# Putting off the gate-and-conv work of the last two up groups, and splitting and fetching the down product's operands in other slots

## The chip, the cores and the metric

The kernel runs on one core of a Trainium2 chip. The metric is the device time of one execution in microseconds (us), from its first to its last instruction and what lies around them; several executions are timed and their median is given. Engines: PE (TensorE, matrix products), DVE (VectorE), ACT (ScalarE), POOL (GpSimd), and SP (SyncE), whose instruction stream issues nearly all transfers (DMAs).

## The reference

One decoder layer on a sequence of 512 positions and width 2048, all in float32:

```python
h = rms_norm(x, norm1_w)
proj = h @ w_in                       # attention heads and an SSM scan follow
x = x + concat([attn, ssm]) @ w_out
h = rms_norm(x, norm2_w)
u = causal_dwconv(h @ w_up, ffn_conv_w, ffn_conv_b)     # 2048 -> 2 * 5632, conv over 3 positions
u_gate, u_val = split(u, 2, axis=-1)
return x + (silu(u_gate) * u_val) @ w_down              # 5632 -> 2048
```

The case is about the last two products, `h @ w_up` (the up product) and `... @ w_down` (the down product), and about the places where one gives way to the next.

## The kernel before

**Precision.** A float32 operand `a` is split into `hi`, a copy in a shorter format that PE takes at full rate (made by ACT), and `lo = a - hi` (made by DVE). A product is then three matmuls: hi·hi, hi·lo, lo·hi.

**Seven products for eight.** Both products are cut in 2 x 2 blocks and done by a scheme with seven products of sums of blocks, named `P1` to `P7`, instead of eight. For each it needs a combination of weight blocks (the left side, one of the tiles `rawa`, `rawb`, or a sum `s` of several, made by DVE and held in PSUM; one sum, in SBUF, `s3`, is made by POOL on line 1027) and a combination of the activations (the right side). The right sides are fixed for many groups; the kernel calls them "kinds" (`KT1, K11, KT2, K21, KT3, K22, KT4`) and holds each as one tile `cmb0` to `cmb6` with hi and lo, with one buffer each.

**Groups and slots.** The up product has 44 groups (`NF = 44`), each a group of output columns with n = 8 blocks of depth. The down product has three passes over the depth (`PASSES`: 7, 8 and 7 pairs of blocks, so n = 7, 8, 7), each with 8 groups. One product of one group is a slot, of 3n matmuls of 128 x 256. `put` (lines 1007 to 1009) interleaves neighbours: seven slots in the order `P5(g), P3(g-1), P1(g), P4(g-1), P6(g), P2(g), P7(g)`. At the first group of a pass the kinds have to be new ones, so each kind's tile is written anew between its last use by the old groups and its first use by the new ones.

**The order of the work.** The slots are issued in order (lines 1284 to 1306), and the order on the other engines is written out by hand: after a slot's matmuls come the reading of its result (`up_after` or `down_after`), and then `step_slot(slot)`: the list `events` of this slot (weight loads, the sums `s2`, `s4`, fetches), `split_lo(slot + 2)` on DVE, the list `after` of this slot (sum `s1`, kind splits, side work), and `split(slot + 3)` on ACT. Each engine works through its own instructions in the order in which they were issued. `base` is the slot of `P5` of the last group before a pass; below, r is a slot's number counted from `base`. There are three such places: from up to pass 0 (base 299), from pass 0 to pass 1 (355), from pass 1 to pass 2 (411).

**The kinds of a pass.** The up product's results, gated and summed into the kinds, lie in DRAM (`gd`). Each kind of a pass is fetched in two halves, so there are 14 halves per pass, numbered q = 0 to 13 in the order of the kinds above: `b_load` (line 1095, on SP) fetches a half into a buffer `ld` (the first two of the first pass into buffers `acc_s`), `b_split` splits it into the kind's tile (ACT line 1106, DVE line 1107). `slots` gives the slots of the splits from `base` on; fetches of the first `early` halves are issued ahead of `base`, the others one slot after the split that frees their buffer.

**Side work.** After `P4` of an up group, `up_side` issues on DVE and ACT what the layer does with the result: scale by the norm (line 1220, 1221), the conv (1198 on ACT, 1199 on DVE), SiLU (1204), gate times value (1210), and for each odd group the sums of a pair (`t_sums`: 888 to 891) and its store to `gd` (line 1067, on SP). It is spread over the seven slots after `P4`, the pair's sums over slots 7 to 10 after it, and 11 (for the last pair 8 and 9) for sums and store.

**Down results.** `down_after` adds a group's seven results up in a buffer (`acc_s` of two, or `acc` of four), and POOL issues a transfer that accumulates it onto `x2d` in DRAM (line 1170). The up product's small tiles lie in a pool `up`, which `down_pool` closes for the pool `down`.

Of the kernel before, what the change touches and what calls it, by code (L numbers as in the profile page):

```python
# [33 lines left out]
NF = FF // 128  # L34
# [17 lines left out]
PASSES = [(0, 7), (7, 8), (15, 7)]  # L52
# [137 lines left out]
def body(ctx, tc, xT, wi, wz, wo, wu, wd0, wd1, wd2, pp, pf, outT, dbg={}):  # L190
# [93 lines left out]
    def pc(name, i=0, n=1):  # L284
        o = _PC[name] + i
        return (p2["par"] if name[0] == "f" else par)[:, o:o + n]
# [513 lines left out]
    for half in range(2):  # L800
        box = {}
# [83 lines left out]
    def sums(E, g, part=None):  # L885

        if part != 1:
            E.tensor_tensor(g[:, 4:6, :], g[:, 1:4:2, :], g[:, 0:2, :], op=OP.subtract)
        if part != 0:
            E.tensor_tensor(g[:, 6, :], g[:, 3, :], g[:, 4, :], op=OP.subtract)  # L890
            E.tensor_tensor(g[:, 7, :], g[:, 2, :], g[:, 6, :], op=OP.subtract)
# [45 lines left out]
    for i in range(4, NK):  # L937
        box = {}
# [41 lines left out]
    ve, se, pe, po, sy = nc.vector, nc.scalar, nc.tensor, nc.gpsimd, nc.sync  # L980
# [3 lines left out]
    def side_tile(pool, shape, name, bufs=1):  # L984
        return pool.tile([128] + shape, F32, name=name, bufs=bufs)
# [13 lines left out]
    items, pos = [], {}  # L999
# [64 lines left out]
    events, after = {}, {}  # L1064

    def at(slot, fn, *args, where=events):
        where.setdefault(slot, []).append(lambda: fn(*args))

    for gi in range(len(groups)):
        p5, p1 = pos[gi, "P5"], pos[gi, "P1"]  # L1070
# [11 lines left out]
    gd = [dram.tile([128, n, 8, 256], F32, name="gd%d" % p) for p, (f, n) in enumerate(PASSES)]  # L1082
# [26 lines left out]
    def down_pool():  # L1109
        up_stack.close()  # L1110
        box["pool"] = ctx.enter_context(tc.tile_pool(name="down", bufs=1, side="right", reuse_waits="tile"))
        box["depth"] = 5

    for p in range(len(PASSES)):
        g0 = NF + 8 * p
        base = pos[g0 - 1, "P5"]
        slots = [2, 4, 5, 7, 8, 9, 9, 10, 11, 11, 12, 13, 14, 15]
        k0 = len(b_list)
        b_list += [(p, t, h) for t in (KT1, K11, KT2, K21, KT3, K22, KT4) for h in range(2)]
        early = 5  # L1120
        for q in range(14):
            at(base + slots[q], b_split, k0 + q, where=after)
        for q in range(14):
            at(base - 6 + q // 2 if q < early else base + slots[q - (5 if p else 3)] + 1, b_load, k0 + q)
        if p == 0:
            at(base + 19, down_pool, where=after)


    x_ld = []

    def x_load(n):
        if n < 4:
            x_ld.append(side_tile(box["pool"], [4, 256], "ld", 3))
            sy.dma_start(x_ld[n], xd[:, 4 * (n % 2):4 * (n % 2) + 4, n // 2, :])

    def x_split(n):
        t, h = (K22, KT4)[n // 2], n % 2
        if h == 0:
            up_kinds[t] = cmb_tile(t)
        o = up_kinds[t][:, :, 4 * h:4 * h + 4, :]  # L1140
        se.activation(o[:, 0], x_ld[n], AF.Copy)
        ve.tensor_tensor(o[:, 1], x_ld[n], o[:, 0].bitcast(F32), op=OP.subtract)
        x_load(n + 3)
# [5 lines left out]
    box = {}  # L1149
# [25 lines left out]
    def up_after(g, x):  # L1175
        X, i = g["X"], g["i"]
        ug, uv = box["ug%d" % (i % 2)], box["uv%d" % (i % 2)]
        if x in ("P1", "P6", "P5"):
            g[x] = side_tile(box["pool"], [256], "c" + x, 2 if x == "P5" else 1)
            se.activation(g[x], X[:, 256:] if x == "P5" else X[:, :256], AF.Copy)  # L1180
        elif x == "P2":
            ve.tensor_tensor(ug[:, 2:258], g["Y"][:, :256], g["P1"], op=OP.add)
        elif x == "P7":
            ve.tensor_tensor(uv[:, 258:514], X[:, :256], g["P5"], op=OP.add)
        elif x == "P3":
            ve.tensor_tensor(ug[:, 258:514], X[:, 256:], g["P6"], op=OP.add)
        else:
            ve.tensor_tensor(uv[:, 2:258], X[:, :256], rbc[:, :256], op=OP.mult)
            up_side(i, ug, uv)

    def up_side(i, ug, uv):
        pool = box["pool"]
        tt = {}

        def conv(u, ci, name, n):
            if n == 0:
                tt[name] = side_tile(pool, [S], name)
                se.activation(tt[name], u[:, 2:514], AF.Identity, bias=pc("fcb", ci), scale=pc("fcw", ci * 3 + 2))
            ve.scalar_tensor_tensor(tt[name], u[:, n:n + S], pc("fcw", ci * 3 + n), tt[name],
                                    op0=OP.mult, op1=OP.add)  # L1200

        def val0():
            conv(uv, NF + i, "tv", 0)
            se.activation(tt["tg"], tt["tg"], AF.Silu)

        def last():
            if i % 2 == 0:
                box["gt"] = side_tile(pool, [8, 256], "gt")
            o = 2 * (i % 2)
            ve.tensor_tensor(box["gt"][:, o:o + 2, :].rearrange("p a b -> p (a b)"), tt["tg"], tt["tv"], op=OP.mult)  # L1210

        def t_sums(n):
            sums(ve, box["gt"], n)
            if n:
                pr = i // 2
                p = max(q for q in range(3) if PASSES[q][0] <= pr)
                at(t0 + (11 if i < NF - 1 else 9), sy.dma_start, gd[p][:, pr - PASSES[p][0]], box["gt"])

        t0 = pos[i, "P4"]
        for d, fn in ((0, lambda: ve.tensor_tensor(ug[:, 2:514], ug[:, 2:514], rbc, op=OP.mult)),  # L1220
                      (1, lambda: ve.tensor_tensor(uv[:, 258:514], uv[:, 258:514], rbc[:, 256:], op=OP.mult)),
                      (3, lambda: conv(ug, i, "tg", 0)), (4, lambda: conv(ug, i, "tg", 1)), (5, val0),
                      (6, lambda: conv(uv, NF + i, "tv", 1)), (6, last)):
            at(t0 + d, fn, where=after)
        if i % 2:
            at(t0 + 7, t_sums, 0, where=after), at(t0 + (10 if i < NF - 1 else 8), t_sums, 1, where=after)

    def down_acc(gi):
        g = groups[gi]
        m, p = g["m"], g["p"]  # L1230
        if gi < NF + 2:
            a = g["acc"] = side_tile(lp, [2, S], "acc_s", 2)
        else:
            a = g["acc"] = side_tile(box["pool"], [2, S], "acc", 4)
        if p == 2:
            sy.dma_start(a, x2d[m])

    for gi, g in enumerate(groups):
        if g["ph"] == "down":
            p5 = pos[gi, "P5"]  # L1240
            at(p5 - 2 if gi == NF else p5 - 5 if gi == NF + 1 else p5 - 2 if gi == NF + 2 else p5 - 6, down_acc, gi,
               where=after)


    up_stack = ExitStack()
# [1 line left out]
    def start_up():  # L1247

        work.close()
        p2["cmb2"] = ctx.enter_context(tc.tile_pool(name="cmb2", bufs=1, side="right", reuse_waits="tile"))  # L1250
        box["pool"] = up_stack.enter_context(tc.tile_pool(name="up", bufs=1, side="right", reuse_waits="tile"))
        box["depth"] = 3
        for n in ("ug0", "uv0", "ug1", "uv1"):
            box[n] = box["pool"].tile([128, 516], F32, name=n)
            ve.memset(box[n][:, 0:2], 0.0)
        x_load(0), x_load(1), x_load(2)
# [27 lines left out]
    for k, (gi, x) in enumerate(items):  # L1284
        g = groups[gi]
        if x == "P5":
            g["X"] = box["ps"].tile([128, 512], F32, name="x")
        if x == "P2":
            g["Y"] = box["ps"].tile([128, 512], F32, name="y")
        out = g["Y"][:, :256] if x == "P2" else g["X"][:, 256:] if x in ("P5", "P3") else g["X"][:, :256]  # L1290
        h, l = parts.pop(k)
        bk = g["kinds"][KIND[x]]
        n = g["n"]
        fresh = x in ("P5", "P2")
        for part in ((range(n - 1), range(n - 1, n)) if k < 2 else (range(n),)):
            for q in part:
                w = h[:, q * 128:(q + 1) * 128]
                pe.matmul(out, w, bk[:, 0, q, :], start=fresh and q == 0, stop=False, skip_group_check=True)  # L1298
                pe.matmul(out, w, bk[:, 1, q, :], start=False, stop=False, skip_group_check=True)  # L1299
            for q in part:  # L1300
                pe.matmul(out, l[:, q * 128:(q + 1) * 128], bk[:, 0, q, :], start=False, stop=q == n - 1,  # L1301
                          skip_group_check=True)
        if k == 0:
            start_up()
        (up_after if g["ph"] == "up" else down_after)(g, x)
        step_slot(k)
# [23 lines left out]
```

## Time and profile before

| | |
|---|---|
| median of 3 runs | 2070.68 us (2070.02 to 2075.01) |
| profiled execution | 2073.51 us, its span 2071.8 us |
| granted PE clock over the span | 0.997 of full speed |
| PE busy | 2037.1 us (98%) |
| DVE busy | 1555.5 us (75%) |
| ACT busy | 1004.8 us (48%) |
| POOL busy | 223.3 us (11%) |
| DMA | 319.79 MB, mean 154 GB/s |

A row of a timeline gives the start, the duration, the engine, the line, and what is written from what; a bracket tells how long the engine stood idle before it, and for whom. On DVE the end of one instruction overlaps the start of the next by about 0.1 us, so the price of an instruction in a busy stretch is the distance from its start to the next one's. A row of a window table gives busy time and count of each engine, the granted PE clock, the share of the DMA engines that was busy, and GB/s. A row of the waits gives total, times and the longest.

### The profile page before, as it was taken

The numbers are of one execution on the slowest core, as the hardware profiler recorded it, in microseconds if no ns is written. First come the engines' busy times: TensorE is split into PE (matmuls) and PEld (weight loads), VectorE is DVE, ScalarE is ACT, GpSimd is POOL, SyncE is SP. The second block draws the span as 40 slices with busy tenths as digits, with TensorE's granted clock in tenths as the row PEclk, the third lists the DMA queues.
The fourth block names the chain that finished last, engine by engine and source line by source line (L and its number), as shares of the span: only waits on it lengthen the run. The fifth ranks groups of instructions, "written<-read, shape, count | busy, mean of one in ns | idle before, by whom it ended". The sixth has DMA issues, their size and how long they took to land.

```text
span 2071.8 us, 37628 instructions
## 1 busy us (share of the span) xinstructions
PE 2037.1 (98%) x15350; PEld 1925.7 (93%) x15350; DVE 1555.5 (75%) x2194; ACT 1004.8 (48%) x1499; POOL 223.3 (11%) x123
## 2 busy tenths in 40 slices
PE   9999999999999998999999999999999899999999
PEld 8889888888888878999999999999999899999999
DVE  6535555345555558999999999999999977967976
ACT  6433435244444435555555555555555644644533
POOL 0020000000000001101110111111011111211210
PEclk9999999999999999999999999999999999999999
DMA  5233222332225545445444444444455667856863
GB/s 196 77 108 94 80 72 82 93 111 83 82 72 168 168 136 193 161 145 194 154 157 180 166 162 162 173 174 163 154 187 203 201 189 213 263 153 215 267 204 122
DMA packets 110940, 319.79 MB, mean 154 GB/s; under 512 B 10352, under 2 KB 34736, under 8 KB 107952
## 3 DMA queue, kind: packets, MB, share of 16 engines
q1 hardware_dynamic: 108464, 309.00, 44.2%
q0 software_dynamic: 2304, 8.39, 2.5%
q8 instruction: 120, 1.97, 0.4%
q14 instruction: 52, 0.43, 0.1%
HBM read 275.38 MB, written 41.98 MB: 153 GB/s over the span
## 4 chain that ended last, share of the span: by engine, by line
PE 92%; DVE 5%; issue 1%; ACT 1%; DMA 1%; SPq 0%; POOL 0%; DVEq 0%; ACTq 0%; POOLq 0%
PE acc L185 31%; PE x L1299 16%; PE x L1298 16%; PE x L1301 16%; PE sm L185 4%; PE y L1298 3%; PE y L1299 3%; PE y L1301 3%; DVE cmb L1107 1%; DVE lo L1060 1%; DMA ld<-gd 0%; DVE lo L185 0%; DMA raw<-wi 0%; ACT hi L1051 0%; DVE t L185 0%
## 5 line engine op out<-in xcount | busy, mean ns | idle before, releaser
L1299 PE MATMUL x<-cmb,hi 128*128 128x256 f32 x3168 | 741.9, 276 | 11.7 <-DVE cmb L1107 10.2
L1298 PE MATMUL x<-cmb,hi 128*128 128x256 f32 x3168 | 741.6, 276 | 10.3 <-ACT cP L1180 5.4
L1299 PEld LDWEIGHTS x<-cmb,hi 128*128 128x128 f32 x3168 | 595.9, 188 | 14.5 <-DVE cmb L1107 12.5
L1298 PEld LDWEIGHTS x<-cmb,hi 128*128 128x128 f32 x3168 | 595.7, 188 | 12.2 <-issue 6.2
L1301 PE MATMUL x<-cmb,lo 128*128 128x256 f32 x3168 | 426.5, 275 | 1.5 <-DVE lo L1060 1.4
L1301 PEld LDWEIGHTS x<-cmb,lo 128*128 128x128 f32 x3168 | 390.5, 188 | 1.9 <-DVE lo L1060 1.9
L185 DVE TENSOR_TENSOR lo<-raw,hi 128x512 fp32r<-128x512 f32 (+1 forms) x240 | 164.4, 691 | 238.0 <-ACT hi L185 228.4
L1051 ACT ACTIVATE hi<-s 128x1024 fp32r<-128x1024 f32 (+1 forms) x201 | 201.1, 1001 | 224.4 <-DVE s L1034 151.7
L1027 POOL TENSOR_TENSOR rawb<-rawa,rawb 128x1024 f32<-128x1024 f32 (+1 forms) x68 | 170.9, 2513 | 1077.0 <-DVE s L1034 894.0
L185 PE MATMUL acc<-A,hi 128*128 128x512 f32 x704 | 278.3, 395 | 0.6 <-ACT hi L185 0.6
L185 PE MATMUL acc<-A,lo 128*128 128x512 f32 x704 | 274.2, 390 | 0.0
L185 PE MATMUL acc<-B,hi 128*128 128x512 f32 x704 | 274.2, 390 | 0.0
L185 ACT ACTIVATE hi<-raw 128x512 fp32r<-128x512 f32 (+1 forms) x240 | 149.2, 629 | 247.3 <-PE acc L185 211.6
L1060 DVE TENSOR_TENSOR lo<-s,hi 128x1024 fp32r<-128x1024 f32 (+1 forms) x201 | 238.7, 1187 | 28.7 <-issue 25.8
L1060 DVE TENSOR_TENSOR lo<-rawa,hi 128x1024 fp32r<-128x1024 f32 (+1 forms) x204 | 242.1, 1187 | 20.3 <-PE x L1301 18.7
L1051 ACT ACTIVATE hi<-rawa 128x1024 fp32r<-128x1024 f32 (+1 forms) x204 | 210.1, 1030 | 12.8 <-PE x L1299 12.7
L185 PEld LDWEIGHTS acc<-A,lo 128*128 128x128 f32 x704 | 132.6, 188 | 28.6 <-DVE lo L185 0.6
L185 PEld LDWEIGHTS acc<-A,hi 128*128 128x128 f32 x704 | 132.9, 189 | 26.3 <-ACT hi L185 0.9
L185 PEld LDWEIGHTS acc<-B,hi 128*128 128x128 f32 x704 | 132.8, 189 | 25.6
L1180 ACT ACTIVATE cP<-x 128x256 f32<-128x256 f32 x132 | 50.8, 385 | 205.1 <-PE x L1301 205.1
L185 PE MATMUL acc<-hi,A 128*128 128x256 f32 (+2 forms) x448 | 134.4, 300 | 0.8 <-DVE u L185 0.8
L185 PE MATMUL acc<-lo,A 128*128 128x256 f32 (+2 forms) x448 | 132.7, 296 | 0.0
(209 smaller groups left out, 2773.6 us busy)
## 6 DMA issues: line engine op xcount, KB each, us to landing
rawa<-wu SPq DMA_DIRECT2D x176, 512.0 KB, 3.7
raw<-wi SPq DMA_DIRECT2D x79, 512.0 KB, 3.6
rawa<-wd SPq DMA_DIRECT2D x64, 448.0 KB, 4.1
rawb<-wu SPq DMA_DIRECT2D x44, 512.0 KB, 4.5
gd<-gt SPq DMA_DIRECT2D x22, 1024.0 KB, 4.4
raw<-wo SPq DMA_DIRECT2D x32, 512.0 KB, 3.7
rawa<-wd SPq DMA_DIRECT2D x32, 512.0 KB, 4.2
ld<-gd SPq DMA_DIRECT2D x27, 512.0 KB, 7.0
```

The costliest lines, as they stand in the source:

```text
L185: return fn(out, *args, **kw)
L1027: po.tensor_tensor(r, raw[gi, "11"][:, :n], r, op=OP.subtract)
L1051: se.activation(h[:, :n], src[:, :n], AF.Copy)
L1060: ve.tensor_tensor(l[:, :n], src[:, :n], h[:, :n].bitcast(F32), op=OP.subtract)
L1107: ve.tensor_tensor(lo, ld[:, :m, :], hi.bitcast(F32), op=OP.subtract)
L1180: se.activation(g[x], X[:, 256:] if x == "P5" else X[:, :256], AF.Copy)
L1298: pe.matmul(out, w, bk[:, 0, q, :], start=fresh and q == 0, stop=False, skip_group_check=True)
L1299: pe.matmul(out, w, bk[:, 1, q, :], start=False, stop=False, skip_group_check=True)
L1301: pe.matmul(out, l[:, q * 128:(q + 1) * 128], bk[:, 0, q, :], start=False, stop=q == n - 1, skip_group_check=True)
```

## The change

Four things are edited.

1. The side work of groups 42 and 43 starts at r = 15 and r = 22 instead of at the `P4` of its group (r = 3 and r = 10). The pair sums of groups 40 and 41 go to r = 13 and 14 (before 3 and 6), their store to r = 15 (before 7); the sums of groups 42 and 43 to r = 29 and 30 (before 17 and 18), the store to r = 31 (before 19).
2. In all three passes the 14 halves are split in the slots 1, 2, 3, 4, 5, 6, 7, 8, 9, 10, 10, 11, 12, 13 instead of 2, 4, 5, 7, 8, 9, 9, 10, 11, 11, 12, 13, 14, 15.
3. Seven halves instead of five are fetched ahead, one for each slot from r = -9 to -3 (before two each in -6 and -5, one in -4). The ring of `ld` has 5 buffers in the pool `up` (before 3) and 7 in the pool `down` (before 5).
4. `down_pool` moves from r = 19 to r = 33. Groups 46 and 47 therefore take the two `acc_s` buffers in turn with groups 44 and 45 (before, they took `acc` buffers); the buffer of a down group is named two slots before its `P5`, in pass 2 six.

```diff
-        box["depth"] = 5
+        box["depth"] = 7
...
-        slots = [2, 4, 5, 7, 8, 9, 9, 10, 11, 11, 12, 13, 14, 15]
+        slots = [1, 2, 3, 4, 5, 6, 7, 8, 9, 10, 10, 11, 12, 13]
...
-        early = 5
+        early = 7
         for q in range(14):
             at(base + slots[q], b_split, k0 + q, where=after)
         for q in range(14):
-            at(base - 6 + q // 2 if q < early else base + slots[q - (5 if p else 3)] + 1, b_load, k0 + q)
+            at(base - 9 + q if q < early else base + slots[q - (7 if p else 5)] + 1, b_load, k0 + q)
         if p == 0:
-            at(base + 19, down_pool, where=after)
+            at(base + 33, down_pool, where=after)
...
-            x_ld.append(side_tile(box["pool"], [4, 256], "ld", 3))
+            x_ld.append(side_tile(box["pool"], [4, 256], "ld", 5))
...
-                at(t0 + (11 if i < NF - 1 else 9), sy.dma_start, gd[p][:, pr - PASSES[p][0]], box["gt"])
-
-        t0 = pos[i, "P4"]
+                at(t2 + (4 if i < NF - 3 else 2), sy.dma_start, gd[p][:, pr - PASSES[p][0]], box["gt"])
+
+        t1 = pos[i, "P4"]
+        if i >= NF - 2:
+            t1 = pos[NF - 1, "P5"] + (15 if i == NF - 2 else 22)
...
-            at(t0 + d, fn, where=after)
+            at(t1 + d, fn, where=after)
         if i % 2:
-            at(t0 + 7, t_sums, 0, where=after), at(t0 + (10 if i < NF - 1 else 8), t_sums, 1, where=after)
+            t2 = t1 + 7 if i != NF - 3 else pos[NF - 1, "P5"] + 13
+            at(t2, t_sums, 0, where=after), at(t2 + (3 if i < NF - 3 else 1), t_sums, 1, where=after)
...
-        if gi < NF + 2:
+        if gi < NF + 4:
             a = g["acc"] = side_tile(lp, [2, S], "acc_s", 2)
...
-            p5 = pos[gi, "P5"]
-            at(p5 - 2 if gi == NF else p5 - 5 if gi == NF + 1 else p5 - 2 if gi == NF + 2 else p5 - 6, down_acc, gi,
-               where=after)
+            at(pos[gi, "P5"] - (6 if g["p"] == 2 else 2), down_acc, gi, where=after)
...
-        box["depth"] = 3
+        box["depth"] = 5
```

## The prediction

> **What bounds the kernel now.** I read the page's busy times first, then who PE waited for, then window by window where it stood still.
>
> ```profile
> PE 2037.1 (98%) x15350; PEld 1925.7 (93%) x15350; DVE 1555.5 (75%) x2194; ACT 1004.8 (48%) x1499; POOL 223.3 (11%) x123
> ...
> PE x L1298 <- ACT cP L1180: 5.4, 2, 5.0
> ...
> PE x L1299 <- DVE cmb L1107: 10.2, 12, 2.0
> PE y L1299 <- DVE cmb L1107: 2.1, 1, 2.1
> PE x L1301 <- DVE lo L1060: 1.4, 1, 1.4
> ...
> 1580.00:1600.00 20.00, 20.00 (x179) 20.00 (x178) 19.07 (x25) 10.65 (x14) 3.45 (x2) 1.00 0.92 307
> ...
> 1620.00:1640.00 20.00, 15.62 (x128) 14.66 (x127) 19.93 (x25) 13.96 (x19) 1.65 (x1) 1.00 0.79 268
> 1640.00:1660.00 20.00, 16.06 (x131) 15.13 (x131) 19.88 (x26) 13.44 (x18) 4.96 (x2) 1.00 0.66 214
> ...
> 1680.00:1700.00 20.00, 20.00 (x179) 20.00 (x178) 14.73 (x18) 8.72 (x13) 4.74 (x3) 1.00 0.67 172
> ```
>
> PE is the bound and full nearly everywhere. The second fence line is its only wait of the up phase (at that phase's start); the next three are nearly all of its waits from 1560 us to the end, and they name the kind splits of line 1107. The windows show why: in the up phase DVE is already busy 19.07 of 20 us, the splits come on top, and from 1620 to 1660 us DVE is full while PE issues 128 and 131 matmuls where 179 fit. In the down groups DVE needs only 14.73 of 20. So near the first place DVE is short for some 50 us, and idle for a quarter of the time after it.
>
> How much is lost in all, from the ends of slots (the lo matmuls are a slot's last third):
>
> ```profile
> 1594.93 1.07 PE L1301 MATMUL x<-cmb,lo 128*128 128x256 f32 x8
> 1597.65 1.07 PE L1301 MATMUL y<-cmb,lo 128*128 128x256 f32 x8
> 1673.56 0.95 PE L1301 MATMUL x<-cmb,lo 128*128 128x256 f32 x7
> 1675.93 0.95 PE L1301 MATMUL x<-cmb,lo 128*128 128x256 f32 x7
> ...
> 1747.34 0.95 PE L1301 MATMUL y<-cmb,lo 128*128 128x256 f32 x7
> 1805.80 1.07 PE L1301 MATMUL y<-cmb,lo 128*128 128x256 f32 x8
> 1901.00 1.07 PE L1301 MATMUL y<-cmb,lo 128*128 128x256 f32 x8
> 1958.84 0.95 PE L1301 MATMUL y<-cmb,lo 128*128 128x256 f32 x7
> ```
>
> An undisturbed slot takes 1597.65 - 1594.93 = 2.72 us with n = 8, and 1675.93 - 1673.56 = 2.38 with n = 7; a matmul 2.72/24 = 0.113, so a slot ends 0.91 or 0.79 after its lo part starts.
> - First place: from r = -2 (1597.65) to r = 24 (1675.93) lie ten slots of 2.72 and sixteen of 2.38, 65.28 us; it took 78.16 from end to end. **12.9 us lost.**
> - Second: r = -2 to 19 (1747.34 to 1805.80): 10 x 2.38 + 11 x 2.72 = 53.72 of 58.58. **4.9 lost.**
> - Third: the same slots (1901.00 to 1958.84): 10 x 2.72 + 11 x 2.38 = 53.38 of 57.73. **4.3 lost.**
>
> Together 22.1 us; no gain can be larger.
>
> **The change part by part.** The sums below use prices from one busy stretch of DVE (start to next start), and three more rows of its lines:
>
> ```profile
> 1609.70 1.23 DVE L1060 TENSOR_TENSOR lo<-s,hi 128x1024 fp32r<-128x1024 f32 x1 [0.56 <-issue]
> 1611.01 1.23 DVE L1107 TENSOR_TENSOR cmb<-acc_s,cmb 128x1024 fp32r<-128x1024 f32 x1
> ...
> 1615.01 0.68 DVE L888 TENSOR_TENSOR gt<-gt 128x512 f32<-128x512 f32 x1
> 1615.61 0.69 DVE L1220 TENSOR_TENSOR ug<-ug,rbc 128x512 f32<-128x512 f32 x1
> ...
> 1652.71 1.24 DVE L1107 TENSOR_TENSOR cmb<-ld,cmb 128x1024 fp32r<-128x1024 f32 x1
> 1653.85 0.76 DVE L1199 SCALAR_TENSOR_TENSOR tg<-ug,par,tg 128x512 f32<-128x512 f32 x1
> 1654.51 0.43 DVE L1162 TENSOR_TENSOR acc_s<-x,acc_s 128x256 f32<-128x256 f32 x1
> 1654.85 1.10 DVE L1060 TENSOR_TENSOR lo<-rawa,hi 128x896 fp32r<-128x896 f32 x1
> 1655.85 0.97 DVE L1107 TENSOR_TENSOR cmb<-ld,cmb 128x768 fp32r<-128x768 f32 x1
> 1656.71 0.76 DVE L1199 SCALAR_TENSOR_TENSOR tv<-uv,par,tv 128x512 f32<-128x512 f32 x1
> ...
> 1663.57 0.42 DVE L890 TENSOR_TENSOR gt<-gt 128x256 f32<-128x256 f32 x1
> 1664.02 2.25 DVE L891 TENSOR_TENSOR gt<-gt 128x256 f32<-128x256 f32 x1
> ```
>
> So: a split of 1024 columns 1.14 (I use 1.13), of 768 0.86; lo, s1, s2, s4 of n = 7 1.00 (n = 8: 1.13, as a split of that size); 256 columns 0.34; a conv step 0.66; 512 columns 0.60. One group's side work is 0.60 + 0.34 + 4 x 0.66 + 0.60 = 4.2 us of DVE, a pair's sums 0.60 + 0.45 + 0.34 = 1.4.
>
> *First place, checked on before.* DVE has caught up at 1609.70, 0.26 after r = 2 ends (1597.65 + 4 x 2.72 + 0.91 = 1609.44), and works without a gap until the last split (q = 13) ends at 1656.71: 47.0 us. That half is wanted 8 matmuls into r = 17: 6 x 2.72 + 8 x 2.38 + 0.91 = 36.3 us after r = 2 ends, at 1645.7. It comes 11.0 us late, of 12.9 lost; the rest is the 1.4 for lo at r = 21, and refills. So this reckoning, DVE's queue against PE's free slots, carries the loss.
>
> *The same with the change.* Out of the 47.0 us go: the split q = 0 (now ahead of r = 2) 1.13; sums of the pair 40/41 1.4; side work of group 42 4.2; of group 43, what stood ahead of q = 13 (0.60 + 0.34 + 2 x 0.66) 2.3; and, since q = 13 moves from r = 15 to 13, what slots 14 and 15 queue (s2, two lo, one add: 3.34). Left 34.6, plus 0.26: q = 13 is done 34.9 us after r = 2 ends, 1.4 early. What is late next is lo, wanted two thirds into its slot. lo of r = 14 (queued in slot 12) has 34.9 - 1.13 - 0.34 - 1.00 - 0.86 = 31.6 ahead and with it, wanted at 6 x 2.72 + 5 x 2.38 + 1.59 = 29.8: 1.8 late. lo of r = 16: 34.9 + 0.60 + 1.00 + 1.00 = 37.5 against 34.6: 2.9 late, the worst. lo of r = 18 has 41.2 against 39.3, of r = 20 43.6 against 44.1: caught up. The put-off work then goes into slots whose own DVE load is 14.73 of 20 us: 17 slots of 2.38 from r = 13 to 30 leave 40 x 0.26 = 10.6 us, and take 4.2 + 4.2 + 2 x 1.4 = 11.2, with lags of lo up to 1.3 on the way, less than PE has already given up. So it is covered, just; were that slack gone, it would cost up to its 11 us. First place: about 3.2 lost (with refills) instead of 12.9: **-9.7**.
>
> *Second and third place* have no side work; there only the slots of the splits change.
>
> ```profile
> 1762.66 1.09 DVE L1060 TENSOR_TENSOR lo<-rawb,hi 128x896 fp32r<-128x896 f32 x1 [1.22 <-issue]
> 1798.14 1.23 DVE L1107 TENSOR_TENSOR cmb<-ld,cmb 128x1024 fp32r<-128x1024 f32 x1
> ...
> 1918.48 1.23 DVE L1060 TENSOR_TENSOR lo<-rawb,hi 128x1024 fp32r<-128x1024 f32 x1 [1.50 <-PE x L1301]
> 1952.35 0.97 DVE L1107 TENSOR_TENSOR cmb<-ld,cmb 128x768 fp32r<-128x768 f32 x1
> ```
>
> Second: r = 4 ends at 1747.34 + 0.79 + 6 x 2.38 = 1762.41. DVE is gapless from 1762.66 to 1799.28 (1798.14 + 1.14); q = 13 is wanted 4 x 2.38 + 8 x 2.72 + 0.91 = 32.2 after r = 4 ends, at 1794.6: 4.7 late, as lost. With the change two splits (q = 1, 2) fall into the idle slots before (2.3), and slots 14 and 15 behind q = 13 (3.7): 30.6 left; q = 13 is in time, lo of r = 16 has 33.1 against 30.4 and is 2.8 late. **-1.9.** Third, likewise: q = 13 ends at 1953.2, wanted at 1949.1 (4.2 late); with the change lo of r = 16 has 31.6 against 29.1, 2.5 late. **-1.7.** Half of each loss stays.
>
> *Fetches.* The seven early ones wait for no buffer; SP passes them among weight loads. DMA was at 0.92 with 307 GB/s in the window that held five of them within three slots; now one per slot is asked for: no cost. The others wait on SP for a split that is queued one slot earlier, as before; weight loads behind them (no engine waited for one here) have four slots and more of lead.
>
> ```profile
> ACT cmb L1106 <- DMA ld<-gd: 6.9, 8, 1.4
> ...
> DMA to landing us min/median/max: 3.1/6.5/9.6
> ```
>
> ACT waited for halves with a ring of three. Now q = 10 to 13 have three slots (7.1 to 7.8 us) from fetch to split: the median lands, the longest would be 2.3 late. I take 0.
>
> *Buffers and stores.* The two stores move past some eight and twelve slots of loads on SP, but each stands one slot behind its sums, as before; with DVE up to 2.9 late SP is held as long, and the weight loads behind have their four slots: 0. Groups 46 and 47 reuse `acc_s` four slots (9.5 us) after the accumulate of 44 and 45 was released; ACT's first copy of 46 would wait if that took longer, and ACT has its hi work three slots ahead: 0. The larger `up` pool shifts tiles where the up phase starts; the nearest row is PE's 5.4 us there, so the bounds are -5.4 and +5.4. I take 0: all that the change moves there is the fourth fetch of x, which with five buffers no longer waits. The later closing of the pool has two slots more than before to its first new tile: 0.
>
> Sum: 9.7 + 1.9 + 1.7 = 13.3 us. The profiled execution took 2073.5 (span 2071.8), so 2060.2 for it; the median of the runs lies 2.8 lower, 2070.7: **2057.4**.
>
> **A place where a rule bears.** At 1664.02 line 891 took 2.25 instead of 0.42, and ended as POOL's subtraction did:
>
> ```profile
> 1663.80 2.19 POOL L1027 TENSOR_TENSOR rawb<-rawa,rawb 128x896 f32<-128x896 f32 x1 [3.49 <-DVE s L1034]
> ```
>
> The Trainium skill, page "SBUF — State Buffer", section "SBUF: two separate sides", says that GpSimd and a VectorE op with two SBUF inputs exclude each other for a whole instruction, whichever starts first. This row agrees, and the put-off work is of just that sort. By the rule alone the sum would lose the price of the second rival; by the rows it loses nothing where DVE's op starts first.
>
> **Rivals.**
> 1. *Halves land late.* q = 10 to 13 by 2.3 us at the first place: 2057.4 + 2.3 = 2060. For it: the ring is still short there; against: those fetches overlap, so it adds once.
> 2. *POOL takes the port first* (the other side). POOL starts its subtraction 0.2 us after each s1, at r = 4, 11, 18, 25. Behind s1 there stand now q = 3, q = 11 and conv steps of 42 and 43. If ACT's half is not ready, DVE has a gap, POOL goes first, and DVE loses 2.25 - 0.42 = 1.8 us. Four times at the first place, twice at each other one: 8 x 1.8 = 14.6 us, 2072.0. It decides from the eighth on; from the fourth the gain is below what can be measured. Against it:
>
> ```profile
> L1106 ACT ACTIVATE cmb<-ld 128x1024 fp32r<-128x1024 f32 (+1 forms) x40 | 39.2, 989 | 10.2 <-DMA ld<-gd 10.2
> ...
> L1160 ACT ACTIVATE acc<-x 128x256 f32<-128x256 f32 x56 | 21.6, 385 | 84.9 <-PE x L1301 84.9
> ```
>
>    ACT needs 0.4 + 1.0 us after the slot's end, DVE's lo and s1 before the split 2.0; and the one row of that kind is a pair's sum, which the change moves off POOL's slots.
> 3. *The change doesn't do what it says:* the put-off work, which leaves no slack (11.2 in 10.6), makes lo late again from r = 18 to 28, and the first place gains only half (4.9): 2062.
>
> **How the numbers follow.** My forecast 0.62 (own range 2054 to 2061: low if the lags of lo are half as large, 4 less); rival 1 0.11; rival 3 0.06 as priced and 0.10 in its worse form, nothing gained at the first place (2067); rival 2 0.11: 0.02 at one to three places, 0.06 at four to eight, 0.03 beyond (POOL's whole 2.2 each time, and on put-off steps later than the first). 0.3% is 6.2 us, about what a measurement of this kernel can tell from no change, so faster is below 2064.5: 0.62 + 0.11 + 0.06 + 0.02 = 0.81; same 0.10 + 0.06 = 0.16; slower 0.03. The range takes the forecast, rivals 1 and 3 and the start of 2, and part of the unknown at the up phase's start: 2053 to 2065.5.
>
> **What would show it.** Right: PE's wait for line 1107 falls from 12.3 us to under 2, and its waits name `lo` of line 1060 instead; about 3 us lost at each place; DVE gapless from r = 3 to beyond r = 25; the store's row of the last pair some 12 slots later. Wrong: waits for `ld<-gd` on ACT of over 2 us each; tg, tv or cmb rows of over 2 us beside POOL; PE waiting at r = 18 to 30.

## The result and the profile after

| | before | after |
|---|---|---|
| median | 2072.07 us (6 runs) | 2061.64 us (6 runs) |
| profiled execution, its span | 2073.51, 2071.8 | 2063.26, 2060.3 |

The change makes the kernel faster: the ratio is 0.9950, 95% interval 0.9937 to 0.9963, or 10.4 us. Forecast were 13.3 us. The three runs of before that the prediction started from had a median of 2070.68, the six 2072.07, so 1.4 of the 4.2 us between the forecast 2057.4 and 2061.64 is the starting point.

Who PE waited for from 1560 us to the end, in the changed kernel (total, times, longest):

```profile
PE x L1299 <- DVE acc L1162: 1.9, 4, 0.6
PE x L1299 <- ACT hi L1051: 1.9, 5, 0.5
PE x L1302 <- DVE lo L1060: 1.1, 3, 0.5
PE x L1299 <- DVE uv L1184: 0.5, 1, 0.5
```

The kind splits (`cmb`, line 1107), 12.3 us of waits before, are gone from the list; lo and hi of the weights and the reading of results stand there, with 5.4 us in all. (PE's lines are one further down than before: 1299, 1300, 1302.) The windows of the first place:

```profile
1580.00:1600.00 20.00, 20.00 (x179) 20.00 (x178) 18.63 (x27) 10.64 (x14) 3.00 (x2) 1.00 0.96 336
...
1620.00:1640.00 20.00, 19.13 (x164) 18.60 (x163) 20.00 (x24) 14.34 (x20) 3.00 (x2) 1.00 0.80 257
1640.00:1660.00 20.00, 18.97 (x158) 18.24 (x159) 18.68 (x25) 11.21 (x16) 5.19 (x3) 1.00 0.72 233
1660.00:1680.00 20.00, 20.00 (x178) 20.00 (x178) 18.68 (x26) 12.32 (x20) 3.39 (x2) 1.00 0.61 171
```

PE issues 164 and 158 matmuls where there were 128 and 131, and DVE carries the put-off work from 1640 on (18.68 of 20 where a down group alone needs 14.73). The early fetches, one per slot, fill the window before (336 GB/s).

The lost time comes out of the same slot ends as in the prediction (r = -2 and 24 at the first place, r = -2 and 19 at the others):

```profile
1598.27 1.07 PE L1302 MATMUL y<-cmb,lo 128*128 128x256 f32 x8
1667.61 0.95 PE L1302 MATMUL x<-cmb,lo 128*128 128x256 f32 x7
...
1739.07 0.95 PE L1302 MATMUL y<-cmb,lo 128*128 128x256 f32 x7
1795.85 1.07 PE L1302 MATMUL y<-cmb,lo 128*128 128x256 f32 x8
1891.05 1.07 PE L1302 MATMUL y<-cmb,lo 128*128 128x256 f32 x8
1947.33 0.95 PE L1302 MATMUL y<-cmb,lo 128*128 128x256 f32 x7
```

First: 1667.61 + 0.79 - 1598.27 - 0.91 - 65.28 = **3.9** (before 12.9). Second: 1795.85 + 0.91 - 1739.07 - 0.79 - 53.72 = **3.2** (4.9). Third: 56.16 - 53.38 = **2.8** (4.3). Together 22.1 became 9.9, which is 12.2 us. The span fell by 11.5, since PE came to r = -2 0.6 us later in this execution (1598.27, before 1597.65); 1.3 us more lay outside the span than in the profiled execution before.

### The profile page after: what moved, and what is told of

The parts are those of the page before. It is cut to its first block, busy times and chain, and to the rows that moved or that the text cites. A ratio compares the mean times of both kernels' runs of the same rounds, so it can differ in the third digit from the quotient of the medians.

```text
span 2060.3 us, 37631 instructions
## 1 busy us (share of the span) xinstructions
PE 2034.6 (99%) x15350; PEld 1924.2 (93%) x15350; DVE 1552.2 (75%) x2194; ACT 1003.1 (49%) x1499; POOL 219.9 (11%) x123
## 5 line engine op out<-in xcount | busy, mean ns | idle before, releaser
L1299 PE MATMUL x<-cmb,hi 128*128 128x256 f32 x3168 | 741.7, 276 | 12.3 <-ACT cP L1180 5.4
L1051 ACT ACTIVATE hi<-rawa 128x1024 fp32r<-128x1024 f32 (+1 forms) x204 | 210.1, 1030 | 12.3 <-PE x L1300 12.3
```

The costliest lines, as they stand in the source:

```text
L1051: se.activation(h[:, :n], src[:, :n], AF.Copy)
```

## The experiments

Theory A: DVE's queue, laid against PE's free slots, sets the loss. Theory B: the ring of three `ld` buffers does, since halves land late. Each run's ratio is to the kernel before on the same chip, and its losses at the three places are worked out as above.

| run | ratio, 95% interval | lost at the places, us |
|---|---|---|
| before | 1 | 12.9, 4.9, 4.3 |
| the whole change | 0.9950 (0.9937 to 0.9963) | 3.9, 3.2, 2.8 |
| e1: side work not put off | 0.9979 (0.9970 to 0.9989) | 12.2, 3.2, 2.8 |
| e2: put off only | 0.9980 (0.9970 to 0.9990) | 8.7, 4.9, 4.3 |
| e3: put off, long rings | 0.9957 (0.9943 to 0.9972) | 4.8, 4.8, 4.3 |
| e4: put off, new split slots | 0.9949 (0.9934 to 0.9964) | 5.5, 3.2, 2.8 |
| e8: long rings only | 0.9993 (0.9983 to 1.0002) | 12.7, 4.8, 4.3 |
| c1: the whole change again | 0.9948 (0.9934 to 0.9961) | 4.1, 3.2, 2.8 |
| e5: last halves a slot later | 0.9939 (0.9927 to 0.9952) | 4.0, 2.6, 2.4 |
| e6: POOL takes two lo, passes 1, 2 | 0.9937 (0.9925 to 0.9950) | 3.9, 2.6, 1.9 |
| e9: POOL takes two lo, all passes | 0.9951 (0.9939 to 0.9964) | 6.0, 4.0, 3.5 |

**e1, the side work back in its place.**

```diff
-        if i >= NF - 2:
-            t1 = pos[NF - 1, "P5"] + (15 if i == NF - 2 else 22)
...
-            t2 = t1 + 7 if i != NF - 3 else pos[NF - 1, "P5"] + 13
+            t2 = t1 + 7
```

> The side work and the pair sums stand again where they stood before; the new split slots, the seven early fetches and the longer rings stay. Theory A (the queue of DVE sets the loss at the first place): 7.8 us of side work stand again ahead of the last halves, lo of r = 16 is 10 us late, the first place loses 11 to 12 us of its 12.9, the second and third keep their gain of 1.7 and 1.6 us: 3.5 to 5 us faster than before. Theory B (the ring of three was the limit, halves landed late): most of the change's gain stays, 9 us or more faster than before.

The first place loses 12.2 again; the others keep their gain. PE's waits from 1590 to 1690 us (total, times, longest):

```profile
PE x L1300 <- DVE lo L1060: 4.5, 6, 1.1
PE x L1297 <- ACT hi L1051: 1.4, 2, 0.9
PE x L1297 <- DVE ug L1186: 1.2, 1, 1.2
```

Splitting and fetching sooner, without the putting off, only moves the wait from the halves to lo. A holds here and B falls.

**e2, putting off alone; e3, with the long rings and early fetches; e4, with the new split slots; e8, rings alone.** Each is the changed kernel with one or two of these parts set back:

```diff
-        slots = [1, 2, 3, 4, 5, 6, 7, 8, 9, 10, 10, 11, 12, 13]
+        slots = [2, 4, 5, 7, 8, 9, 9, 10, 11, 11, 12, 13, 14, 15]    # e2, e3, e8
...
-        early = 7
+        early = 5           # e2, e4, with ld rings of 3 and 5 and the fetch slots of before
...
-        if i >= NF - 2:     # e8, as e1
```

> Only the side work is put off (with the later closing of the pool that this needs); split slots, early fetches and rings as before. Theory A: q = 13 has 39.4 us of DVE ahead against 36.3, so the first place loses 3.5 to 4 us instead of 12.9, the other two stay: 9 us faster than before. Theory B: halves still come through a ring of three with 6.5 us of landing, the first place loses 8 to 9 us: 4 us faster.

> Side work put off, long rings and seven early fetches, but the old split slots. Theory A: as e2_putoff_only within 1 us, 9 us faster than before; the second and third place lose 4.9 and 4.3 us as before. Theory B: clearly faster than e2_putoff_only, by 4 us or more.

> Side work put off and the new split slots, but the old rings (3 and 5) and five early fetches. Theory A: as the whole change, 10 to 12 us faster than before. Theory B: with a ring of three a half is fetched only one or two slots (2.4 to 4.8 us) ahead of its split and lands in 6.5, so each late half holds ACT and DVE 2 us or more: 5 to 8 us of the first place's gain are gone, 3 to 6 us faster than before.

> Only the longer rings and the seven early fetches, with the later closing of the pool; side work and split slots as before. Theory A with the fetch as the second limit behind it (halves late by the fetch only show once DVE has time): the first place still loses 11 to 13 us, the others 4.9 and 4.3 as before: no change, within 2 us of before. Theory B (the fetch is a cost of its own beside DVE's): 3 to 4 us faster, as much as the rings gave once the side work was put off.

e2 is a miss for A, which said 9 us: it is 0.9980, 4 us, and the first place loses 8.7, as B said. First e2's waits there, of ACT and PE, then PE's in e3:

```profile
ACT cmb L1106 <- DMA ld<-gd: 4.1, 3, 1.9
...
PE x L1300 <- DVE cmb L1107: 2.9, 2, 1.6
PE y L1299 <- ACT cmb L1106: 0.9, 1, 0.9
```

```profile
PE x L1300 <- DVE cmb L1107: 2.3, 3, 1.4
PE x L1299 <- DVE acc_s L1162: 0.9, 1, 0.9
```

With DVE relieved, PE waits even for ACT's half of a split, and ACT for the transfer. With a ring of three a half is fetched one slot after the split three halves earlier. In the old slots, where halves stand close (9, 9, 10, 11, 11), that leaves one slot, 2.4 to 2.7 us, for a landing of 5.8 us in the median of e2. The long rings take 3.9 us off (e3, 4.8; by the ratios 4.8 us, so B is right on this pair too). But on the kernel before they are worth nothing (e8): DVE was full there anyway, and the first limit hid the second.

In e2's execution the granted PE clock also fell, to 0.55 and 0.50 of full speed from 1639 to 1646 us. That is not what the 8.7 are made of: DVE's split of the last half (q = 13), wanted 36.3 us after r = 2 ends, ends 44.8 us after it (1652.62, against 1607.80), 8.5 late, and DVE shows no idle time from 1640 until then for which a slower PE could be the cause.

e4 is a miss for B: with the new slots, about one half per slot, the ring of three leaves two slots for most halves (one for q = 10 to 12), and though ACT still waits,

```profile
ACT cmb L1106 <- DMA ld<-gd: 5.2, 3, 2.5
```

the first place loses 5.5, 1.5 more than with all parts. So either remedy, rings or evenly spread slots, is enough for most of it once the side work is out of the way; the timed ratios of e3, e4 and the whole don't tell the three apart, the slot ends do. The gain at the second and third place comes from the slots alone (4.9 to 3.2 in e1 and e4; 4.8 in e3 and e8).

**c1, the changed kernel again, and e5, the last halves later:**

```diff
-        slots = [1, 2, 3, 4, 5, 6, 7, 8, 9, 10, 10, 11, 12, 13]
+        slots = [1, 2, 3, 4, 5, 6, 7, 8, 9, 10, 11, 12, 14, 14]
```

> The changed kernel once more, as the measure for the others of this group: 10 to 11 us faster than before; 3.9, 3.2 and 2.8 us lost at the three places.

> The changed kernel with the last halves a slot later: split slots 1 to 10, 11, 12, 14, 14. Theory A (deadlines of DVE's queue): in the changed kernel q = 13 comes 1.4 us early while lo of r = 14 and 16 come 1.8 to 2.9 late, so halves moved behind lo of r = 14 to 16 even that out: second place 3.2 to about 2.0 us lost, third 2.8 to 1.8, first the same or 0.2 better; 2 to 2.5 us faster than the changed kernel. Rival (the splits are simply best as early as possible, or the rest is ACT and PSUM waits): the same or 1 us slower than the changed kernel.

c1 repeats the change (0.9948). e5 has 0.9939, with an interval that overlaps c1's; by the slot ends it wins 0.6 at the second place and 0.4 at the third; at the first (4.0) it is within what two executions of the change differ by (3.9 and 4.1). The direction is A's, the size half of it: at the first place r = 14 and 15 lose 0.8 instead of 1.9, but r = 17 now 2.0 instead of 0.5. PE's row at the start of r = 17:

```profile
1644.84 0.35 PE L1299 MATMUL x<-cmb,hi 128*128 128x256 f32 x1 [1.71 <-DVE acc_s L1162]
```

It waits for DVE to read a result (line 1162), and that reading stands behind the two later splits and a pair's sums. In neither order does all that DVE has to do in this stretch come in time; that no order does is not shown.

**e6 and e9, POOL takes two subtractions.** e6 has the slots of the change, e9 gives POOL the last kind in all passes and has split slots 1 to 10, 11, 12, 12, 13.

```diff
-        ve.tensor_tensor(lo, ld[:, :m, :], hi.bitcast(F32), op=OP.subtract)
+        (po if p and t == KT4 else ve).tensor_tensor(lo, ...)      # e6; e9: (po if t == KT4 else ve)
```

> The changed kernel, but in passes 1 and 2 POOL instead of DVE subtracts the lo of the last two halves (q = 12, 13). Theory A alone (only the length of DVE's queue counts): DVE is 2.3 and 2.0 us shorter there, lo of r = 16 is late by 0.5 instead of 2.8, 1 to 1.5 us faster than the changed kernel. Rival (POOL and DVE exclude each other where DVE reads two SBUF operands): each POOL subtraction (2.2 to 2.5 us alone) holds up DVE's lo of raw tiles, with rows of over 2 us on line 1060 or 1107, or waits 2 us and more itself and makes the half late: 1 to 5 us slower than the changed kernel.

> The changed kernel with split slots 1 to 10, 11, 12, 12, 13, and POOL subtracts the lo of the last two halves in all three passes. Theory A (length of DVE's queue up to lo of r = 16): the first place is relieved too, 3.9 to about 2.5 us lost, second 2.3, third 1.9: 3 us faster than the changed kernel, 13 to 14 faster than before. Rival (the port): POOL's subtraction, the longer for DVE being full, holds up side work and lo of raw tiles at the first place, or the half comes after r = 17 has begun: first place 4 to 6 us, nothing gained on the changed kernel.

Each shows the port (POOL and DVE excluding each other). First POOL's two subtractions and DVE's row beside them in e6, then the same in e9:

```profile
1778.60 4.78 POOL L1107 TENSOR_TENSOR cmb<-ld,cmb 128x1024 fp32r<-128x1024 f32 x2
...
1781.47 2.99 DVE L1060 TENSOR_TENSOR lo<-rawa,hi 128x1024 fp32r<-128x1024 f32 x1
```

```profile
1638.65 4.88 POOL L1107 TENSOR_TENSOR cmb<-ld,cmb 128x1024 fp32r<-128x1024 f32 x2
...
1638.93 2.91 DVE L1107 TENSOR_TENSOR cmb<-ld,cmb 128x768 fp32r<-128x768 f32 x1
```

In both a DVE instruction with two operands in SBUF lasts 1.8 and 2.0 us longer (2.99 instead of 1.2, 2.91 instead of 0.95), while those that read PSUM beside it have their usual length. In e6 DVE's shorter queue outweighs that: the second and third place lose 2.6 and 1.9 (c1: 3.2 and 2.8), against the rival's expectation. In e9, with its later slots, the held-up instruction is the last half that r = 15 needs, and the reading of a result, for which r = 15 waits too, stands right behind it:

```profile
1642.32 0.41 PE L1299 MATMUL x<-cmb,hi 128*128 128x256 f32 x1 [2.17 <-DVE acc_s L1162]
```

At the first place r = 15 loses 3.9. Only some 2.4 of that are the wait: from 1642.3 to 1645.3 the granted PE clock is 0.53, the hi matmuls start 0.21 us apart instead of 0.113, and 14 of them take 1.4 us more. At the second and third place, at full clock, r = 15 loses 2.8 and 2.6. So the same hold-up costs nothing or some 2.5 us, by what it falls on, and e9 gains nothing on the change (0.9951 against c1's 0.9948), as the rival said. e5 and e6 are the two fastest versions, 1.5 to 2 us below c1 by the medians (2057.96 and 2058.42 against 2059.92), with overlapping intervals.

**e7, sums beside POOL.**

```diff
-            t2 = t1 + 7 if i != NF - 3 else pos[NF - 1, "P5"] + 13
+            t2 = t1 + 7 if i < NF - 3 else pos[NF - 1, "P5"] + (13 if i == NF - 3 else 31)
```

> The changed kernel with the sums of the last pair (groups 42, 43) two slots later, at r = 31 and 32, so that line 891 stands behind s1 and a 256-column sum again, when POOL starts its subtraction, as it did in the kernel before. If POOL's start at that point took the port: the last row of line 891 is 2.0 to 2.4 us long instead of 0.43. If the long row was chance: 0.43. The time stays in either case, within 2 us of the changed kernel, since DVE has slack there.

```profile
1686.94 2.18 POOL L1027 TENSOR_TENSOR rawb<-rawa,rawb 128x896 f32<-128x896 f32 x1 [3.12 <-DVE s L1034]
...
1686.70 0.42 DVE L890 TENSOR_TENSOR gt<-gt 128x256 f32<-128x256 f32 x1
1687.15 2.25 DVE L891 TENSOR_TENSOR gt<-gt 128x256 f32<-128x256 f32 x1
```

The long row is back to within 0.01 us. It was no chance: POOL starts while the short op of line 890 runs, has the port when line 891 comes, and holds it to its end. The same row has 2.25 us in e1 and e8 too, where the sums stand in their old place. The time, from one run, is 2060.36 (c1 2059.92), and up to r = 24 the losses are c1's. But the slack of DVE doesn't take up the hold-up whole, as was expected: behind it lo of r = 28 comes late,

```profile
1691.79 1.09 PE L1302 MATMUL x<-cmb,lo 128*128 128x256 f32 x7 [0.84 <-DVE lo L1060]
```

and from r = 26 to 33 PE takes 17.8 us for seven slots of 2.38, 16.7, so 1.1 us are lost that the changed kernel doesn't lose there.

## Why the prediction was right

*First place: 9.7 forecast, 8.9 measured.* DVE's queue came out as reckoned. r = 2 ends at 1609.15 + 0.91 = 1610.06; DVE works without a gap until lo of r = 16 and beyond, and that lo ends at 1647.89, 37.8 us later where 37.5 were reckoned: 3.3 late instead of 2.9. By the slot ends r = 8 to 16 lose 3.3 us together. PE's rows there (the bracket is its idle time), then two of DVE's:

```profile
1623.96 0.36 PE L1299 MATMUL x<-cmb,hi 128*128 128x256 f32 x1 [0.49 <-DVE uv L1184]
...
1642.02 1.08 PE L1302 MATMUL x<-cmb,lo 128*128 128x256 f32 x7 [0.27 <-DVE lo L1060]
1643.57 0.36 PE L1299 MATMUL x<-cmb,hi 128*128 128x256 f32 x1 [0.48 <-ACT hi L1051]
```

```profile
1643.01 0.42 DVE L1162 TENSOR_TENSOR acc_s<-x,acc_s 128x256 f32<-128x256 f32 x1
...
1646.81 1.08 DVE L1060 TENSOR_TENSOR lo<-rawa,hi 128x896 fp32r<-128x896 f32 x1
```

The path was named only in part. The prediction's sign was that PE's waits name `lo`; lo has 1.1 of the 5.4 us. Most of the loss is a wait that the sum did not have: the reading of results. At r = 8 PE waits until DVE has read the result of `P7` (line 1184), which stands behind the early splits, and starts 0.14 us after it. r = 10, 15 and 17 also start 0.14 us after a result has been read. (The row at r = 15, 1643.57, names an ACT instruction that ended at that moment, but ACT had made hi of r = 15 by 1642.00; DVE's reading on line 1162 ended at 1643.43.) By the slot ends these four slots lose 2.5 us, and r = 14 and 16, by hi and lo, 1.4. What PE loses on the way makes the next wait shorter, so up to r = 16 all of it together is no more than the 3.3 by which lo of r = 16 is late. The last reading comes behind that lo, and r = 17 loses 0.5 more by it. So of the 3.9, 3.3 are a queue that was reckoned right to 0.4 us, and 0.5 a deadline that the sum left out: it set them for halves and lo only. The 0.3 that it allowed for refills covered part of that.

*Second and third place: 1.9 and 1.7 forecast, 1.7 and 1.5 measured.* Here too DVE's queue came out: at the second place lo of r = 16 ends 33.3 us after r = 4 (reckoned 33.1). About two thirds of each loss stay (3.2 of 4.9, 2.8 of 4.3), which fits the prediction's sums (3.0 and 2.6 would have stayed) better than its "half".

*The put-off work.* Forecast was that it just fits (11.2 us into 10.6). It fits with room: DVE already waits for PE at r = 18 and 25.

```profile
1654.30 1.09 DVE L1060 TENSOR_TENSOR lo<-rawb,hi 128x896 fp32r<-128x896 f32 x1 [1.29 <-PE x L1302]
...
1671.04 1.09 DVE L1060 TENSOR_TENSOR lo<-rawb,hi 128x896 fp32r<-128x896 f32 x1 [1.28 <-PE x L1302]
```

The sign "gapless beyond r = 25" was wrong; the other one, that PE would be seen waiting at r = 18 to 30, did not come (0.1 us lost, at r = 24). The slack was too small for two reasons. The window of 20 us (14.73 busy, 0.26 free) is not a whole number of groups: over one group of the kernel before, 1700 to 1716.66, DVE is busy 11.61 of 16.66, 0.30 free. And the busy share counts the end of each instruction, part of which overlaps the next, while the work was summed from start to start; in that measure a down group takes 7 x 1.00 + 3 x 1.00 + 3 x 0.34 = 11.0 of its 16.7 us, a slack of 0.34. Rival 3 lived on the 0.26.

*The fetches at 0* were right for the whole change: no row of ACT waiting for `ld<-gd` is left, although the median landing of all halves rose from 6.5 to 7.4 us and the longest from 9.6 to 12.1. e2 shows what this 0 rested on. With the rings and the split slots of before, the step that counted DVE's queue alone would have been 5 us off (with the rings alone of before, e4, 1.5), a limit that the prediction saw in before (6.9 us of ACT's waits) and priced only as rival 1.

*Rival 2, the port,* did not come in the changed kernel, for the reason given: the conv step starts right behind s1 and POOL is the one that waits.

```profile
1656.31 0.74 DVE L1199 SCALAR_TENSOR_TENSOR tg<-ug,par,tg 128x512 f32<-128x512 f32 x1
...
1656.55 2.51 POOL L1027 TENSOR_TENSOR rawb<-rawa,rawb 128x896 f32<-128x896 f32 x1 [2.91 <-DVE s L1034]
```

POOL's subtraction takes 2.51 instead of 2.19. The rule of the Trainium skill, page "SBUF — State Buffer", section "SBUF: two separate sides", whoever starts first holds the pair for the whole instruction, agrees with this row, with e7's 2.25 and with e6's and e9's 2.9 to 3.0.

The port does have a part in the gain, though. In the kernel before the long row of line 891 stood ahead of lo of r = 21, for which PE waited 1.4 us; by the slot ends 1.7 us are lost there. e1 and e8, which keep the sums in their old place, lose 1.4 and 1.6 at the same slot behind the same long row; the changed kernel loses nothing there. So some 1.7 of the 9 us gained at the first place come from the pair's sums no longer standing where POOL starts. The prediction had them in its sum as "the 1.4 for lo at r = 21", without that cause.

## What to carry to other kernels

Where two stages meet on an engine that is nearly full, lay its queue end to end against the other engine's free slots, with a deadline for everything that the other waits for, the reading of its results too; work without a deadline goes behind the crowd. Relieving the first limit shows the second (here a fetch ring), so test the parts of a change alone and in pairs: rings alone gave nothing, putting off alone 4 us, either pair with it 9 to 10. And take slack and work in the same measure.

## What was not expected of the hardware

Short waits of PE cost more than their rows show: in the changed kernel 4.1 us of waits lie in the three places (the other 1.2 or so come after 2050 us), against 9.9 us lost. At r = 14 the rows show 0.29 and 0.27, the slot is 1.05 longer. Most of that difference is in how rows are counted: a matmul's row lasts 0.28 us, the next one starts 0.113 after it, so some 0.17 of each wait lie under the row before, and the first matmul after a wait is followed 0.2 us later instead of 0.113. That is 0.27 for each of the eleven waits, 3 us in all; much of the rest are waits too short to get a bracket, as at r = 10 and 17.

Nor was it expected that the granted PE clock would fall to about half after a pause as short as 2.2 us: for some 3 us in e9, and for some 6 in e2 after several waits of 0.6 to 1.6. In e9 pauses just as long at the second and third place, and in the kernel before waits of 2.07 and 1.96, left it at 1.00. What decides is open.

That POOL's hold on DVE could be brought back to 0.01 us (2.25 and 2.25 us) by placing one instruction was not expected either.
